# State-space stage of a hybrid decoder: decays spread over the partitions by DMA and masked on GpSimd, in place of one-hot and mask matmuls

## The chip, the cores and the metric

The kernel runs on one core of a Trainium2 chip. The metric is the device time of one execution in microseconds (us), the median of several runs. The core's engines run side by side, each through its own fixed order of instructions: TensorE (PE in the profile, its weight loads PEld), VectorE (DVE), ScalarE (ACT), GpSimd (POOL) and SyncE (SP), which issues nearly all DMAs. SBUF is the memory on the core with 128 partitions, PSUM the one that matmuls write.

## What is computed

The reference is a decoder trunk of two layers on 512 tokens with 1024 features: a Mamba-2 mixer with a dense mixer, and a sparse attention with a dense mixer. The change lies in the Mamba-2 mixer, in the scan over chunks of 256 tokens:

```python
def step(state, inp):
    xk, bk, ck, dtk = inp
    acs = jnp.cumsum(dtk * A, axis=1)
    seg = acs[:, :, None, :] - acs[:, None, :, :]
    decay = jnp.exp(jnp.where(causal[None, :, :, None], seg, -jnp.inf)).reshape(bsz, L, L, G, J)
    xdt = (xk * dtk[..., None]).reshape(bsz, L, G, J, p_dim)
    cb = jnp.einsum("blgn,bsgn->blsg", ck, bk)
    y_intra = jnp.einsum("blsg,blsgj,bsgjp->blgjp", cb, decay, xdt)
    y_inter = jnp.einsum("blgn,bgjpn->blgjp", ck, state) * jnp.exp(acs).reshape(bsz, L, G, J)[..., None]
    ...
```

There are 32 heads of 64 features in four groups, and two chunks. For each head and chunk the matrix `decay` holds exp(acs[target] - acs[source]) for all targets that are not before their source. The factor exp(acs[target]) of `y_inter` is wanted for the second chunk alone, since the state starts at zero.

## The kernel before

The kernel is written with a tile framework: the program names tiles from pools with a fixed number of buffers and the operations on them, and the framework puts the instructions of each engine into a fixed order, sets the waits and gives out buffers. All matrices of weights come from memory in units of 128 x 1024 (`Weights`, `split_unit`, lines 41 to 127): SP issues the load into one of four `raw` buffers, ACT copies it to the upper part (L112), DVE subtracts for the lower part (L113), and each unit feeds 24 matmuls of 512 columns (`mm3`, L133 to L135): an eighth of the unit by three products each.

`mamba` (line 517) makes the input projection for the steps and the first five tiles of group 0, and then goes through four groups `g` of eight heads. For each group it projects six tiles (B, C and four tiles of x, each of two heads), puts them through the convolution, and calls `ssd` (line 595). In group 0 the generator `steps` (line 454) makes, beside this, the cumulated decays `acs` of all heads with tokens on partitions, their negatives `nacs`, and `acsT`: 64 rows, the decays of the 32 heads split exactly into an upper part and a lower part, each with all 512 tokens (transposes L511, copy L514).

In `ssd` the exponent acs[target] - acs[source] is needed with sources on partitions and targets along the free dimension. The part -acs[source] is a column and is the bias of the exponential. The part acs[target] is a row that all 128 partitions need, and here PE spreads it: a matmul with a column of the one-hot matrix `oh`, repeated 128 times, as weights and `acsT` as the moving side writes the row of head `hd` into all partitions of a PSUM bank `sa` (L645, 512 columns), and once more its second halves of the chunks into a bank `sb` (L650, 256 columns). The causal mask, 0 or -1e30, is added to the diagonal blocks by four more matmuls of an identity with `mask_t` in bf16 (L647 and L652). ACT then takes four exponentials from PSUM into the tile `m` (L656 twice 256 columns, L659 twice 128), and DVE multiplies `m` by `cb`, the product of C and B (L661). `m` is what PE multiplies by the inputs `xd` (L667, L671). For the state's part, L674 multiplies state and C, and L675 spreads the two heads' rows of the second chunk over 64 partitions each, with weights `ohp`, for the exponential L677. This goes on in four pairs of heads `j`; ahead of a pair's last steps its gate is projected (`gate`, 24 matmuls, L592). Then come the norm and the splits, and after group 3 the output projection (`project_out`, L276 to L278).

Tiles of up to 4 KB a partition come from the pool `b4` with 33 buffers (`big`), smaller ones from `t2` with 8 (`tmp`). All loads of weights, of modulation rows (`mod`, L159) and of x are issued by SP in one order.

Of the kernel before, what the change touches and what calls it, by code (L numbers as in the profile page):

```python
# [9 lines left out]
F32 = mybir.dt.float32  # L10
F32R = mybir.dt.float32r
# [6 lines left out]
P = 128  # L18
S = 512
# [21 lines left out]
class Weights:  # L41
    """A matrix as a stream of 128x128 blocks, eight to a transfer, each split exactly in two."""
# [21 lines left out]
    def held(self):  # L64
        """The next eight blocks, to be kept for longer."""
        assert self.left == 0
        hi, lo = self.kern.split_unit(self.dram[self.unit], held=True)
        self.unit += 1
        return [(hi[:, i * P:(i + 1) * P], lo[:, i * P:(i + 1) * P]) for i in range(8)]


class Kernel:
# [19 lines left out]
    def banks(self, n, i=0):  # L92
        """n banks to accumulate in; of two or four, the ones of i differ."""
# [14 lines left out]
    def split(self, hi, lo, src, bias=None):  # L108
        """hi + lo is src (+ bias) with all of its bits, each part exact in float32r."""
# [27 lines left out]
    def linear(self, weights, x, ps=None):  # L137
        """One tile of 128 output features; x is a list of (hi, lo) per input tile."""
# [6 lines left out]
    def linear_start(self, weights, x, count, parts):  # L145
        """The first tiles of output features, token part by token part, as their inputs come."""
# [8 lines left out]
    def mod(self, n, behind=False):  # L155
        """Modulation columns 128 n.. : silu(c) @ mod_w + mod_b."""
# [17 lines left out]
    def scale_cols(self, gain, mod0, plus):  # L174
        """gain * (plus + modulation) as columns."""
# [5 lines left out]
    def rsqrt(self, sums, n):  # L181
        """1 / sqrt(sums / n + eps) of a few columns."""
# [20 lines left out]
    def rstd(self, sums, n):  # L203
        """1 / sqrt(mean + eps) of sums of squares [feature lane, token], on all partitions, in PSUM."""
# [10 lines left out]
    def unit_rows(self, x, out):  # L215
        """out[t] = x[t] * rstd, for a few tiles of tokens [token, feature]; written over with squares before."""
# [16 lines left out]
    def turned(self, xn, k, count=1):  # L233
        """Feature tiles k.. of rows, with features on partitions, in PSUM."""
# [8 lines left out]
    def modulate(self, h, src, scale, shift, k, sl):  # L243
        """h = (hi, lo) of src * scale + shift."""
# [8 lines left out]
    def rows(self, cols):  # L253
        """Columns of features as rows of 1024, on all partitions."""
# [17 lines left out]
    def mm3_rows(self, ps, x, t, wh, wl, start, stop):  # L272
        """Adds to ps, [token, 512 features], what input tile x gives for token tile t."""
# [6 lines left out]
    def project_out(self, dram, x, x_src, gain, x_dst, first=None, after=None, mods=(), held=()):  # L280
        """x_src + gain * rmsnorm(x @ weights), [token, feature]. The second half of the features is done in two
        token parts, and what follows on a part (after) goes on while the other is multiplied. Without first, both
        halves of the features are."""
# [29 lines left out]
        for i in range(2):  # L313
# [19 lines left out]
            # one token tile ends before the other  # L333
# [62 lines left out]
    def before(self, gain, mod0, keep=None):  # L396
        """What follows on the residual stream: the modulated norm, to go on with; and its tiles."""
# [46 lines left out]
    def conv(self, ps, j):  # L444
        """Causal convolution of four taps of channel tile j."""
# [8 lines left out]
    def steps(self, ps, c):  # L454
        """softplus, cumulated decays and what hangs on them, from the raw steps [32 heads, tokens]."""
# [45 lines left out]
        sp = self.tmp((P, 4, 2, 32), F32R)  # L501
        nc.scalar.activation(sp[:, :, 0], acs, AF.Copy)
        nc.vector.tensor_tensor(out=sp[:, :, 1], in0=acs, in1=sp[:, :, 0].bitcast(F32), op=OP.subtract)
# [6 lines left out]
        for b in range(4):  # L510
            nc.tensor.transpose(pt[0:64, b * P:(b + 1) * P], sp[:, b].rearrange("p a h -> p (a h)").bitcast(F32),  # L511
                                self.ident)
        self.acsT = self.keep.tile([64, 512], F32R, name="acsT")
        nc.scalar.activation(self.acsT, pt[0:64, :], AF.Copy)  # L514
        self.dt = dt

    def mamba(self, x, x_src, x_dst):
        nc = self.nc
        with ExitStack() as es:
            self.keep = es.enter_context(self.tc.tile_pool(name="ssm", bufs=1))  # L520
            c = self.constants(CST_M, "cst_m")
            self.mask_t = self.keep.tile([P, P], BF16, name="mask_t")
# [664 lines left out]
```

## Time and profile before

| | before |
|---|---|
| median of 3 runs | 1565.19 us (1564.48 to 1568.77) |
| span of the profiled execution | 1564.4 us |
| PE busy | 1515.3 us, 97% |
| DVE busy | 989.5 us, 63% |
| ACT busy | 701.9 us, 45% |
| POOL busy | 20.4 us, 1% |
| DMA | 226.11 MB, mean 145 GB/s |

The profile gives the span, from the first instruction to the last, as the time of its own execution. Matmuls overlap each other, so that the busy time of a group of matmuls is more than the time it keeps PE; the distance between two starts tells that. The groups' idle time is the time that their engine stood still ahead of them, with who ended the wait.

### The profile page before, as it was taken

What the parts mean: (1) busy time and instruction counts of PE and PEld (TensorE: products, weight loads), DVE (VectorE), ACT (ScalarE), POOL (GpSimd) and SP (SyncE); (2) the same over time, 40 slices, a digit from 0 to 9 for tenths busy, and PEclk for the clock granted to TensorE, in tenths of its full rate; (3) what the DMA queues carried; (4) which work ended last, traced back from release to release, by engine and by line L of the source; (5) the groups of instructions that cost most, each with busy time, mean ns of one, the idle gap of its engine ahead of it and who ended that gap; (6) DMA issues with size and microseconds to landing.
All of it is one profiled execution on the core that took longest, in us unless ns stands there. A gap on an engine that the chain in (4) does not pass through costs nothing.

```text
span 1564.4 us, 20765 instructions
## 1 busy us (share of the span) xinstructions
PE 1515.3 (97%) x8014; PEld 1216.9 (78%) x8014; DVE 989.5 (63%) x1800; ACT 701.9 (45%) x1228; POOL 20.4 (1%) x27
## 2 busy tenths in 40 slices
PE   6999999999999999999999989999999999999997
PEld 4767676777889788888878877777688888888886
DVE  7856676778585788872367578888856333333246
ACT  4564746565364222322356465655645332222243
POOL 0000000000000000000000100000000000000000
PEclk9999999999999999999999999999999999999999
DMA  8422141334763888873466443122144122232254
GB/s 303 152 68 68 41 135 46 117 121 156 257 211 109 280 296 285 297 269 101 167 215 210 108 149 94 48 75 68 42 175 149 41 95 94 95 106 95 95 202 148
DMA packets 65125, 226.11 MB, mean 145 GB/s; under 512 B 7809, under 2 KB 9345, under 8 KB 65026
## 3 DMA queue, kind: packets, MB, share of 16 engines
q1 hardware_dynamic: 64738, 224.53, 43.5%
q8 instruction: 63, 1.03, 0.3%
q14 instruction: 36, 0.29, 0.1%
q10 hardware_dynamic: 288, 0.25, 0.1%
HBM read 204.83 MB, written 8.39 MB: 136 GB/s over the span
## 4 chain that ended last, share of the span: by engine, by line
PE 77%; DVE 9%; DMA 8%; ACT 3%; issue 2%; SPq 1%; POOL 0%; DVEq 0%; ACTq 0%; POOLq 0%
PE acc L133 12%; PE acc L134 12%; PE acc L135 12%; PE seg L276 5%; PE seg L278 5%; PE seg L277 5%; PE acc L278 3%; PE acc L276 3%; PE acc L277 3%; DMA raw<-in_mod_dram 2%; DMA raw<-in_ffn_in_dram 2%; DVE w L113 2%; PE mi L1036 2%; DMA b<-b 2%; PE acc L1053 2%
## 5 line engine op out<-in xcount | busy, mean ns | idle before, releaser
L113 DVE TENSOR_TENSOR w<-raw,w 128x1024 fp32r<-128x1024 f32 x233 | 288.0, 1237 | 260.0 <-ACT w L112 259.3
L112 ACT ACTIVATE w<-raw 128x1024 fp32r<-128x1024 f32 x233 | 245.9, 1057 | 369.4 <-PE seg L278 120.5
L133 PE MATMUL acc<-b,w 128*128 128x512 f32 x976 | 386.0, 397 | 3.2 <-DVE t L450 1.0
L134 PE MATMUL acc<-b,w 128*128 128x512 f32 x976 | 384.0, 393 | 0.0
L135 PE MATMUL acc<-b,w 128*128 128x512 f32 x976 | 383.5, 393 | 0.1
L133 PEld LDWEIGHTS acc<-b,w 128*128 128x128 f32 x976 | 183.3, 188 | 43.1 <-issue 4.1
L135 PEld LDWEIGHTS acc<-b,w 128*128 128x128 f32 x976 | 183.7, 188 | 39.8 <-issue 1.7
L134 PEld LDWEIGHTS acc<-b,w 128*128 128x128 f32 x976 | 183.8, 188 | 36.9 <-issue 0.7
L160 DVE SCALAR_TENSOR_TENSOR raw<-raw,b 128x1024 f32<-128x1024 f32 x112 | 136.1, 1221 | 19.1 <-DMA raw<-in_mod_dram 18.4
L276 PE MATMUL seg<-w,b 128*128 128x512 f32 x340 | 132.9, 391 | 0.0
L278 PE MATMUL seg<-w,b 128*128 128x512 f32 x340 | 132.7, 390 | 0.0
L277 PE MATMUL seg<-w,b 128*128 128x512 f32 x340 | 132.4, 389 | 0.0
L1005 ACT ACTIVATE b<-seg,nm 128x512 f32<-128x512 f32 (+3 forms) x128 | 66.0, 525 | 52.5 <-DVE nm L1000 49.8
L112 ACT ACTIVATE b<-t 128x512 fp32r<-128x512 f32 (+1 forms) x108 | 55.2, 529 | 47.8 <-DVE t L426 38.5
L277 PEld LDWEIGHTS seg<-w,b 128*128 128x128 f32 x340 | 63.8, 188 | 13.3
L278 PEld LDWEIGHTS seg<-w,b 128*128 128x128 f32 x340 | 63.8, 188 | 13.2
L276 PEld LDWEIGHTS seg<-w,b 128*128 128x128 f32 x340 | 63.9, 188 | 12.7
L426 DVE TENSOR_TENSOR t<-t,acc 128x512 f32<-128x512 f32 x40 | 27.4, 685 | 63.3 <-PE acc L135 63.3
L425 ACT ACTIVATE t<-acc 128x512 f32<-128x512 f32 x40 | 23.7, 593 | 95.3 <-PE acc L135 95.3
L113 DVE TENSOR_TENSOR b<-t,b 128x512 fp32r<-128x512 f32 (+1 forms) x108 | 59.2, 567 | 9.2 <-ACT b L112 8.9
L277 PE MATMUL acc<-w,b 128*128 128x512 f32 x164 | 64.0, 390 | 0.0
L278 PE MATMUL acc<-w,b 128*128 128x512 f32 x164 | 64.0, 390 | 0.0
(300 smaller groups left out, 2390.1 us busy)
## 6 DMA issues: line engine op xcount, KB each, us to landing
raw<-in_mod_dram SPq DMA_DIRECT2D x112, 512.0 KB, 4.5
raw<-in_ffn_in_dram SPq DMA_DIRECT2D x88, 512.0 KB, 4.5
raw<-in_ffn_out_dram SPq DMA_DIRECT2D x66, 512.0 KB, 3.3
raw<-in_ssm_in_dram SPq DMA_DIRECT2D x41, 512.0 KB, 3.4
raw<-in_ssm_out_dram SPq DMA_DIRECT2D x24, 512.0 KB, 4.3
b<-b SPq DMA_DIRECT2D x32, 256.0 KB, 4.5
raw<-in_kv_dram SPq DMA_DIRECT2D x12, 512.0 KB, 4.2
raw<-in_q_dram SPq DMA_DIRECT2D x9, 512.0 KB, 5.5
```

The lines of the kernel that those rows point to most:

```text
L112: nc.scalar.activation(hi, src, AF.Copy)
L113: nc.vector.tensor_tensor(out=lo, in0=src, in1=hi.bitcast(F32), op=OP.subtract)
L133: nc.tensor.matmul(ps, wh, xh, start=start, stop=False)
L134: nc.tensor.matmul(ps, wh, xl, start=False, stop=False)
L135: nc.tensor.matmul(ps, wl, xh, start=False, stop=stop)
L160: i = nc.vector.scalar_tensor_tensor(out=raw, in0=raw, scalar=1.0, in1=self.cs, op0=OP.mult, op1=OP.mult, accum_out=self.modc[:, n:n + 1])
L276: nc.tensor.matmul(ps, x[0][:, ts], wh, start=start, stop=False)
L277: nc.tensor.matmul(ps, x[0][:, ts], wl, start=False, stop=False)
L278: nc.tensor.matmul(ps, x[1][:, ts], wh, start=False, stop=stop)
L1005: nc.scalar.activation(p[i], bank[:, at:at + n], AF.Exp, bias=nm[:, i:i + 1], accum_out=d[:, i:i + 1])
L1036: nc.tensor.transpose(ps[:, i * n + a * P:i * n + (a + 1) * P], unit["p"][j * per + i][:, a * P:(a + 1) * P], self.ident)
L1053: self.nc.tensor.matmul(po[64 * i:64 * i + 64, bs], vt[a][:, r * 256 + kv * 64:r * 256 + kv * 64 + 64], unit["w"][2 * i + r][:, a * P:(a + ...
```

## The change

The one-hot matrix, `ohp`, `acsT` and the bf16 mask go. `steps` transposes `acs` itself into 32 rows, copies them to `at` and stores them in memory (`acsd`, 32 x 512, 64 KB). A new function `exponents` makes, for a head, a tile of 768 columns: SP loads the head's row of 512 tokens from memory onto all 128 partitions (256 KB written), and GpSimd makes two adds of 256 elements each, the second halves of the chunks with the mask into columns 512 to 767, and the first halves with the mask in place. `ssd` calls it for the first two heads at its start and for the pair j + 1 at the start of pair j. The four exponentials of a head then go from this tile into itself. The rows for the state's part are loaded for the whole group into one tile `ea` (two loads of 64 partitions with 4 KB each) and put through one exponential of 1024 columns. The pools keep their sizes; the mask now stays in the tile of constants. Comments that the diff also takes out are left out here.

```diff
@@ steps
-        sp = self.tmp((P, 4, 2, 32), F32R)
-        nc.scalar.activation(sp[:, :, 0], acs, AF.Copy)
-        nc.vector.tensor_tensor(out=sp[:, :, 1], in0=acs, in1=sp[:, :, 0].bitcast(F32), op=OP.subtract)
...
-            nc.tensor.transpose(pt[0:64, b * P:(b + 1) * P], sp[:, b].rearrange("p a h -> p (a h)").bitcast(F32),
-                                self.ident)
-        self.acsT = self.keep.tile([64, 512], F32R, name="acsT")
-        nc.scalar.activation(self.acsT, pt[0:64, :], AF.Copy)
+            nc.tensor.transpose(pt[0:32, b * P:(b + 1) * P], acs[:, b], self.ident)
+        at = self.tmp((32, 512))
+        nc.scalar.activation(at, pt[0:32, :], AF.Copy)
+        self.acsd = self.dram.tile([32, S], F32, name="acsd")
+        nc.sync.dma_start(self.acsd, at)
@@ mamba
-            self.mask_t = self.keep.tile([P, P], BF16, name="mask_t")
-            nc.vector.tensor_copy(out=self.mask_t, in_=c("mask_t"))
-            self.oh = self.keep.tile([64, 32], F32R, name="oh")
-            nc.scalar.activation(self.oh, c("onehot")[0:64], AF.Copy)
@@ new
+    def exponents(self, hd, c):
+        nc = self.nc
+        e = self.big((P, 768))
+        nc.sync.dma_start(e[:, 0:512], self.acsd[hd:hd + 1, :].to_broadcast([P, 512]))
+        v = e[:, 0:512].rearrange("p (k b l) -> p k b l", k=2, b=2)
+        mask = c("mask_t")[:, None, :].to_broadcast([P, 2, P])
+        nc.gpsimd.tensor_tensor(out=e[:, 512:768].rearrange("p (k l) -> p k l", k=2), in0=v[:, :, 1], in1=mask,
+                                op=OP.add)
+        nc.gpsimd.tensor_tensor(out=v[:, :, 0], in0=v[:, :, 0], in1=mask, op=OP.add)
+        return e
@@ ssd
+        es = [self.exponents(8 * g + i, c) for i in range(2)]
+        ea = self.big((P, 4, 256))
+        for i in range(2):
+            nc.sync.dma_start(ea[64 * i:64 * i + 64],
+                              self.acsd[8 * g + i:8 * g + 8:2, 256:512][None].to_broadcast([64, 4, 256]))
+        nc.scalar.activation(ea, ea, AF.Exp)
...
-        ohp = self.tmp((64, 8, 64), F32R)
-        nc.scalar.activation(ohp, self.oh[:, 8 * g:8 * g + 8, None].bitcast(F32).to_broadcast([64, 8, 64]), AF.Copy)
-        ohp = ohp.rearrange("p (j i) d -> p j (i d)", i=2)
...
-            sb = self.seg()
-            for i in range(2):
+            now = es
+            es = [self.exponents(8 * g + 2 * j + 2 + i, c) for i in range(2)] if j < 3 else []
+            for i, m in enumerate(now):
                 hd = 8 * g + 2 * j + i
-                sa = self.seg()
-                oh = self.oh[:, hd:hd + 1].to_broadcast([64, P])
-                nc.tensor.matmul(sa, oh, self.acsT, start=True, stop=False)
-                for k in range(2):
-                    nc.tensor.matmul(sa[:, k * 256:k * 256 + P], self.identb, self.mask_t, start=False, stop=k == 1)
-                v = sb[:, i * 256:(i + 1) * 256].rearrange("p (k l) -> p k l", k=2)
-                a2 = self.acsT.rearrange("p (k b l) -> p k b l", k=2, b=2)[:, :, 1]
-                nc.tensor.matmul(v, oh, a2, start=i == 0, stop=False, skip_group_check=True)
-                for k in range(2):
-                    nc.tensor.matmul(v[:, k], self.identb, self.mask_t, start=False, stop=k == 1,
-                                     skip_group_check=True)
-                m = self.big((P, 768))
-                for k in range(2):
-                    nc.scalar.activation(m[:, k * 256:(k + 1) * 256], sa[:, k * 256:(k + 1) * 256], AF.Exp,
-                                         bias=self.nacs[:, 2 * k, hd:hd + 1])
-                for k in range(2):
-                    nc.scalar.activation(m[:, 512 + k * P:512 + (k + 1) * P], v[:, k], AF.Exp,
-                                         bias=self.nacs[:, 2 * k + 1, hd:hd + 1])
+                for at, n, b in ((0, 256, 0), (256, 256, 2), (512, 128, 1), (640, 128, 3)):
+                    nc.scalar.activation(m[:, at:at + n], m[:, at:at + n], AF.Exp, bias=self.nacs[:, b, hd:hd + 1])
                 nc.vector.tensor_tensor(out=m, in0=m, in1=cb, op=OP.mult)
...
-            nc.tensor.matmul(pi[:, 256:512], ohp[:, j], self.acsT[:, 256:512], start=True, stop=True)
-            ea = self.tmp((P, 256))
-            nc.scalar.activation(ea, pi[:, 256:512], AF.Exp)
-            nc.vector.tensor_tensor(out=ea, in0=ea, in1=pi[:, 0:256], op=OP.mult)
+            nc.vector.tensor_tensor(out=ea[:, j], in0=ea[:, j], in1=pi[:, 0:256], op=OP.mult)
```

## Rows read from the trace of the kernel before

**Rows 1.** The page: the span, and in 40 slices PE busy and its granted clock.

```profile
span 1564.4 us, 20765 instructions
...
PE   6999999999999999999999989999999999999997
...
PEclk9999999999999999999999999999999999999999
```

**Rows 2.** The chain that ended last, 86 to 385 us: shares by line.

```profile
by line: PE acc L134 19.1%; PE acc L133 19.0%; PE acc L135 19.0%; PE mi L667 7.9%; PE seg L645 4.1%; PE mi L674 3.4%; PE seg L650 3.1%; PE mi L671 2.9%; PE mi L620 2.5%; PE seg L652 2.3%; PE mi L630 2.3%; PE seg L647 2.2%; PE mi L675 1.7%; 
```

**Rows 3.** Groups of instructions of PE, 86 to 385 us: line, operands, count | busy, mean | idle before.

```profile
L133 PE MATMUL acc<-b,w 128*128 128x512 f32 x248 | 99.5, 401 | 1.0 <-DVE t L450 1.0
```

**Rows 4.** Stretches: length, busy us (count) of PE, PEld, DVE, ACT, POOL; clock, DMA share, GB/s.

```profile
155.40:239.10 83.70, 83.70 (x407) 60.16 (x406) 57.58 (x93) 49.19 (x82) 0.00 (x0) 1.00 0.27 88
155.40:202.10 46.70, 46.70 (x238) 30.52 (x236) 26.99 (x38) 33.34 (x63) 0.00 (x0) 1.00 0.12 42
...
322.90:369.80 46.90, 46.90 (x244) 31.42 (x242) 36.43 (x59) 34.44 (x63) 0.00 (x0) 1.00 0.41 132
369.80:400.00 30.20, 30.20 (x144) 25.14 (x144) 25.94 (x54) 11.72 (x15) 0.32 (x1) 1.00 0.61 202
```

**Rows 5.** Instructions of PE in order of time, from 123 us: start, length, line.

```profile
123.03 0.50 PE L645 MATMUL seg<-acsT,oh 64*128 64x512 f32 x1
123.45 0.28 PE L647 MATMUL seg<-mask_t,identb 128*128 128x128 bf16 x2
123.67 0.38 PE L650 MATMUL seg<-acsT,oh 64*128 64x256 f32 x1
123.98 0.28 PE L652 MATMUL seg<-mask_t,identb 128*128 128x128 bf16 x2
124.20 0.49 PE L645 MATMUL seg<-acsT,oh 64*128 64x512 f32 x1
```

**Rows 6.** The same, from 343.9 us: the first of six, and the next head's.

```profile
343.92 0.50 PE L645 MATMUL seg<-acsT,oh 64*128 64x512 f32 x1
...
344.79 0.38 PE L650 MATMUL seg<-acsT,oh 64*128 64x256 f32 x1
```

**Rows 7.** The same, around the first L675.

```profile
97.30 0.38 PE L675 MATMUL mi<-acsT,t 64*128 64x256 f32 x1
97.52 0.39 PE L645 MATMUL seg<-acsT,oh 64*128 64x512 f32 x1
```

**Rows 8.** Instructions of ACT in order of time, 81 to 90 us.

```profile
81.95 0.58 ACT L514 ACTIVATE acsT<-mi 64x512 fp32r<-64x512 f32 x1
...
88.63 0.84 ACT L656 ACTIVATE b<-seg,nacs 128x256 f32<-128x256 f32 x2
89.36 0.63 ACT L659 ACTIVATE b<-seg,nacs 128x128 f32<-128x128 f32 x2
```

**Rows 9.** DMA issues: tiles, engine, count, size of each, median us to landing.

```profile
out_dram<-b SPq DMA_DIRECT2D x8, 256.0 KB, 2.0
b<-b SPq DMA_DIRECT2D x32, 256.0 KB, 4.5
b<-t SPq DMA_DIRECT2D x16, 64.0 KB, 2.0
```

**Rows 10.** Instructions of POOL and DVE in order of time, near 882 and 979 us.

```profile
881.96 1.63 POOL L706 TENSOR_TENSOR t<-t,b 128x512 f32<-128x512 f32 x1 [2.87 <-DVE t L705]
882.36 2.31 DVE L113 TENSOR_TENSOR w<-raw,w 128x1024 fp32r<-128x1024 f32 x1
...
978.78 1.28 POOL L706 TENSOR_TENSOR t<-t,b 128x512 f32<-128x512 f32 x1 [24.73 <-DVE t L705]
```

**Rows 11.** Instructions of PE in order of time: the first products of the first pair.

```profile
96.09 0.65 PE L667 MATMUL mi<-b,b 128*64 128x256 f32 x2
```

**Rows 12.** Groups of instructions of DVE, 155.4 to 239.1 us: splits of weights and products.

```profile
L113 DVE TENSOR_TENSOR w<-raw,w 128x1024 fp32r<-128x1024 f32 x10 | 12.2, 1217 | 0.0
L661 DVE TENSOR_TENSOR b<-b,b 128x768 f32<-128x768 f32 x8 | 7.7, 957 | 8.5 <-ACT b L659 8.5
```

More of the change, by code (lines that the diff above doesn't have):

```diff
@@ L683, in ssd @@
                                            op0=OP.mult, op1=OP.add)
-            nc.vector.tensor_tensor(out=y[:, 256:512], in0=y[:, 256:512], in1=ea, op=OP.add)
+            nc.vector.tensor_tensor(out=y[:, 256:512], in0=y[:, 256:512], in1=ea[:, j], op=OP.add)
             z = zs[j] if j < len(zs) else self.gate(w, h, self.tmp())
@@ L1078 @@
                      ("dt_bias", 1), ("pe_k", 16), ("pe_v", 16)])
-CST_M, _ = _places([("tri", 128), ("mask_t", 128), ("onehot", 32)])
+CST_M, _ = _places([("tri", 128), ("mask_t", 128)])
 CST_A, _ = _places([("mask_q", 128), ("add_pe", 128), ("cmp_add", 128), ("cmp_ok", 128)])
@@ L1087, in _constants @@
     ok = ((16 * cc + 31 <= t) & (cc < 31)).reshape(P, 128)
-    m = [i[:, None] <= i[None, :], np.where(i[:, None] <= i[None, :], 0.0, NEG),
-         i[:, None] % 32 == np.arange(32)[None, :]]
+    m = [i[:, None] <= i[None, :], np.where(i[:, None] <= i[None, :], 0.0, NEG)]
     q = [np.where(i[None, :] <= i[:, None], 0.0, NEG), np.eye(P) + (i[:, None] == 31), np.where(ok, 0.0, NEG), ok]
```

## The prediction

> **What bounds the kernel now.** I read the page first. The span is 1564.4 us, and the median of the runs shown is 1565.19, so the profiled execution stands for them within 0.8 us and I make the sum against 1565. The row of TensorE (PE) in the 40 slices stands at 9 nearly everywhere, and its granted clock at 9 throughout, the upper of its two levels [rows 1]. That is only a busy share, so the next view is the chain of waits, cut to the state-space stage, 86 to 385 us: if the matmuls that the change removes lie on the chain there, their time is worth its full amount. They do. L645, L650, L652, L647 and L675 hold 4.1 + 3.1 + 2.3 + 2.2 + 1.7 = 13.4% of these 299 us, 40.1 us [rows 2]. The grouped view of the same stretch says how idle PE was: one of its 25 groups of matmuls shows idle time ahead of it, 1.0 us, waiting for VectorE (DVE), and the others show none [rows 3]. So here PE sets the end, and it never waits for what the change makes faster or slower. The third view is the stretches by engine. One group of eight heads takes 83.7 us, with PE busy in all of it, DVE in 57.58 and ScalarE (ACT) in 49.19. Inside it the part with the heads (155.4 to 202.1) is 46.7 us, with ACT at 33.34 [rows 4]. These are the loads that must still fit once PE is shorter.
>
> **What is removed on PE.** For each of the 32 heads go one 512-column and one 256-column matmul against the one-hot rows and four bf16 mask matmuls; for each of the 16 pairs of heads goes the 256-column product with ohp. Matmuls overlap, so a duration is no price; the price is the distance between starts. Where the six run in one piece, the next head's L645 starts at 124.20 after 123.03: 1.17 us [rows 5]. Where PE comes from other work and goes on, the six take 343.92 to 344.79: 0.87 us [rows 6]. L675 takes 97.30 to 97.52: 0.22 us [rows 7]. So 32 x 0.87 + 16 x 0.22 = 31.4 us, or 32 x 1.17 + 3.5 = 40.9 us. The chain says 40.1. I take 38, nearer the chain, since it counts all of them in their places. The four transposes of steps stay (32 rows in place of 64).
>
> **What is removed elsewhere.** On ACT: a copy and a split per group and the four exponentials of L677, which one 1024-column exponential per group replaces; on DVE one subtraction of the split. I price these at nothing, since PE is late there and not these engines. The 32 x 4 exponentials keep their sizes and read SBUF in place of PSUM; two of 256 columns take 0.84 us and two of 128 take 0.63, 1.47 us a head [rows 8].
>
> **What is added.** (1) One 64 KB store of the cumulated decays, 32 loads of 256 KB that repeat a 2 KB row on 128 partitions, and eight more of 256 KB (two a group, 64 partitions each) for ea, all on SP's queue. The bytes are 40 x 256 KB = 10.5 MB over the 299 us, 35 GB/s on top of the 42 to 202 GB/s that its stretches move, at a DMA share of 0.12 to 0.61 [rows 4], so the engines have room. What counts is latency: a 64 KB load landed after 2.0 us, 256 KB ones after 2.0 and 4.5 us [rows 9]. No row shows a row repeated from memory; the bounds are 2.0 and 4.5 and I take the later one, as that form is also a load to SBUF. (2) Two adds of 256 elements on GpSimd (POOL) per head, 64 in all. The only adds before are 512 wide and took 1.28 us at their shortest and 1.63 us in the case that the first rival looks at [rows 10]. Bounds: half of the former, 0.64, and the whole, 1.28; I take 0.7, because half the elements is the nearer row. The Trainium skill, GPSIMD Engine Reference, section 4.1, advises against adds on GpSimd, about twice as slow as VectorE; its 4497 ns for 2048 elements with the 1.28 us above gives an estimate of 0.74 us, and the sum would be the same. With 0.7, POOL works 16 x 0.7 = 11 us of a group of some 75 us, and is no bound by itself.
>
> **What the path pays.** In the first group the decays come later. Now acsT is ready at 81.95 + 0.58 = 82.53. The store (2.0), the load (4.5), two adds of the first head (1.4), its exponentials (1.5) and its product (0.96) make 10.4 us: 92.9, and the second head another 1.5, by ACT; the present first product of the pair starts at 96.09 [rows 8, 11]. The removed matmuls of three heads (3 x 1.17 = 3.5 us) lie ahead of that, so PE would want to start it near 92.6: 0 to 3 us late, with gate matmuls as cover. I take 1. In the later groups the pair of heads ahead is loaded while the present one is multiplied (some 9 us), against 4.5 + 2.8 us for load and adds; cover holds, price nothing. If it failed it would cost that chain, below. What SP has queued behind a waiting load are weight loads; they have four raw and three split buffers, up to seven units ahead of PE with 24 matmuls each, so a wait of some us is covered. Then the tighter fit: with 38/4 = 9.5 us less in a group, ACT has 33 us in a part of 37 us, and DVE 27 us plus what GpSimd holds up. PE's order is fixed and it will wait now and then; I put 1.5 us a group on this, 6 in all. It is bounded by nothing and by the second rival. Last, in the fourth group DVE is already at 36.43 of 46.9 and then 25.94 of 30.2 us [rows 4]; I add 1 us for GpSimd there.
>
> Sum: 1565 - 38 + 1 + 6 + 1 = 1535 us.
>
> **Rivals.** *VectorE and GpSimd take turns, and VectorE becomes the bound (slower).* The trace shows the mechanism: with a GpSimd add from 881.96 to 883.59, the split L113, which starts at 882.36, takes 2.31 us where its mean in the state-space group is 1.22; it ends 1.08 us after the add [rows 10, 12]. The Trainium skill, SBUF — State Buffer, section "SBUF: two separate sides", calls this an exclusive lock for the whole instruction between GpSimd and a VectorE instruction with two SBUF inputs; the trace agrees, 2.31 against 1.22 us. Here ten such splits and eight products a group take 12.2 + 7.7 us, with smaller ones besides [rows 12], so an add meets one perhaps half the time. If every add stopped DVE for its whole length p, a group would need 57.58 + 16p: 68.8 us at 0.7, still below PE's 74; it reaches the present 83.7 at p = 1.63, the contended price of an add twice as wide. At that p the first three groups gain nothing and the last stretch, 322.9 to 400, needs 36.43 + 25.94 + 26 = 88 in place of 77.1: +11, or 1576 us. Over all four the loss overtakes the gain from p = 1.45 on: 3 x (83.7 - 57.58 - 16p) + (77.1 - 62.37 - 16p) is zero there. Against it: half the width, and half the meetings.
>
> *The part with the heads stays bound by ScalarE's chain (half the gain).* ACT is busy 33.34 of 46.7 us there; if PE runs out of gate matmuls and the next group's are not moved in, the part shrinks only to about 42 us in place of 37: 4 x 4.5 = 18 us of the 38 are lost, and 1565 - 38 + 18 + 2 = 1547. For it: the exponentials, squares, gates and splits share ACT, and all of PE's cover is in a fixed order. Against it: exponentials no longer wait for PE at all.
>
> *The full gain.* If nothing waits, 1565 - 40 = 1525.
>
> *The prefetch does not happen.* The shared pool of 33 big tiles now holds ea, the constants and two more pairs of heads for longer. If the next pair waits for the present one's tiles, the chain per pair is 4.5 + 2.8 + 2.9 + 1.9 = 12.1 us against 9 of PE, and four of them 48.4 us, in place of 46.7 now: 1565 + 4 x 1.7 = 1572 if it is so everywhere. In the last group alone, where most tiles are held, it loses 9.5 + 1.7: 1535 + 11 = 1546.
>
> **How the numbers follow.** Forecast 1535 with its own range 1528 to 1542: 0.50. Half the gain or a prefetch lost in the last group, 1542 to 1558: 0.25. The full gain, 1523 to 1528: 0.09. Within 0.3% of 1565, about what a measurement of this kernel can tell from no change (1560.5 to 1569.9), by a larger share of the same losses: 0.06. Slower, by VectorE or the prefetch: 0.10. So faster 0.84, same 0.06, slower 0.10, and 1524 to 1556 holds 8 in 10.
>
> **What would show it.** Right: the stretch from the first head group to the last is some 30 us shorter, PE still at 9 in its slices, POOL with 64 adds near 0.7 us, everything behind 400 us merely shifted. Lock: products and splits of the stage well above 0.957 and 1.217 us, and idle PE time ahead of the matmuls that read the products, put down to DVE. ScalarE: PE idle put down to ACT within the heads. Prefetch: GpSimd waiting on DMA each pair, and SP waiting on the products. The forecast is wrong if added PE idle time in the stage exceeds 15 us, or if code behind the stage falls into another order.

## The result, and the profile after

The changed kernel takes 1555.4 us (median of 4 runs, 1552.1 to 1556.5) beside 1564.8 us for the kernel before on the same chip: a ratio of 0.9933, interval 0.9909 to 0.9956. That is 10 us faster, a third of the 30 us forecast. It lies outside the forecast's own range (1528 to 1542) and just inside the upper end of the wide one (1524 to 1556).

The page of the changed kernel (its span; TensorE and GpSimd in 40 slices) against [rows 1]:

```profile
span 1554.3 us, 20592 instructions
...
PE 1485.1 (96%) x7806; PEld 1204.2 (77%) x7806; DVE 997.8 (64%) x1798; ACT 710.3 (46%) x1216; POOL 83.2 (5%) x91
...
PE   6999899999999999999999999999999999999998
...
POOL 0040303040000000000000100000000000000000
```

Among the first nine slices, which hold the stage, one 8 in the row of PE is all that the page shows; GpSimd's busy time now stands in four of the first nine slices, one for each group of heads. The gain is made within the stage and stays: the first matmul of the next projection, L276, starts at 355.9 us in place of 365.8, and the last matmul of all at 1546.2 in place of 1555.9.

The chain that ended last, 81 to 378 us, shares by line (the view cuts its own line), against [rows 2]:

```profile
by line: PE acc L133 11.5%; PE acc L134 11.3%; PE acc L135 11.0%; DMA b<-acsd 7.1%; PE mi L664 5.2%; issue 4.2%; DVE w L113 2.6%; DVE b L680 2.4%; DVE raw L160 2.3%; DVE b L658 2.3%; DVE b L676 2.2%; DVE t L450 2.2%; DMA raw<-in_mod_dram 2.
```

The three lines of the linear matmuls fell from 57% to 34% of the chain. It was PE alone; now it runs through VectorE and the loads of the rows as well, so TensorE alone no longer sets the end.

Groups of TensorE's instructions, 76 to 376 us (line, operands, count | busy, mean ns | idle before, and what ended it), against [rows 3]:

```profile
L133 PE MATMUL acc<-b,w 128*128 128x512 f32 x248 | 102.2, 412 | 10.0 <-ACT w L112 4.3 <-DVE t L450 2.5 <-ACT t L587 2.3
...
L664 PE MATMUL mi<-b,b 128*64 128x256 f32 x128 | 31.0, 391 | 3.5 <-DVE b L658 3.0 <-issue 0.4
...
L208 PE MATMUL mi<-ones,ssq 128*128 128x1 f32 x32 | 5.6, 297 | 2.8 <-DVE ssq L684 2.8
```

The idle time ahead of L133 went from 1.0 to 10.0 us, and most of it waits for ScalarE: for the split of weights (L112) and for a gate (L587).

Stretches of the second group of heads (length, busy us of PE, PEld, DVE, ACT, POOL; clock, DMA share, GB/s), against the first two of [rows 4]:

```profile
149.20:231.60 82.40, 76.54 (x356) 57.91 (x355) 59.12 (x93) 51.45 (x80) 14.59 (x16) 0.96 0.40 122
149.20:191.20 42.00, 38.82 (x199) 27.30 (x197) 28.29 (x40) 37.36 (x62) 14.59 (x16) 1.00 0.35 97
```

The part with the heads shrank by 4.7 us, but ScalarE is busy in 37.36 of its 42.0 us, where it had 33.34 of 46.7. The whole group shrank by only 1.3 us, and the granted clock is no longer 1.00 in it.

Of the 4.0 us that ScalarE has more, 3.8 are table loads, 10 in place of 7 (one stands wherever ScalarE goes over between a Silu and the exponentials). The groups of its instructions in that part, before (155.4 to 202.1 us) and after (149.2 to 191.2):

```profile
L656 ACT ACT_TABLE_LOAD x3 | 3.8, 1283 | 0.1
L592 ACT ACT_TABLE_LOAD x3 | 3.8, 1283 | 0.1
...
L659 ACT ACT_TABLE_LOAD x1 | 1.3, 1283 | 0.0
```

```profile
L657 ACT ACT_TABLE_LOAD x4 | 5.1, 1283 | 0.1
L587 ACT ACT_TABLE_LOAD x4 | 5.1, 1283 | 0.1
...
L573 ACT ACT_TABLE_LOAD x1 | 1.3, 1283 | 0.0
L612 ACT ACT_TABLE_LOAD x1 | 1.3, 1283 | 1.0 <-DMA b<-acsd 1.0
```

Here is the end of that part, TensorE first, then ScalarE (start, length, line, [idle before <- what ended it]):

```profile
188.70 0.38 PE L668 MATMUL mi<-b,b 128*64 128x128 f32 x2
191.24 0.50 PE L133 MATMUL acc<-b,w 128*128 128x512 f32 x1 [2.16 <-ACT w L112]
191.58 0.39 PE L134 MATMUL acc<-b,w 128*128 128x512 f32 x1
193.39 1.87 PE L208 MATMUL mi<-ones,ssq 128*128 128x1 f32 x8 [1.42 <-DVE ssq L684]
195.12 0.77 PE L133 MATMUL acc<-b,w 128*128 128x512 f32 x1
195.70 0.63 PE L134 MATMUL acc<-b,w 128*128 128x512 f32 x1
196.12 0.63 PE L135 MATMUL acc<-b,w 128*128 128x512 f32 x1
```

```profile
178.52 1.28 ACT L587 ACT_TABLE_LOAD   x1
179.81 0.60 ACT L587 ACTIVATE t<-acc 128x512 f32<-128x512 f32 x1
180.43 1.28 ACT L657 ACT_TABLE_LOAD   x1
181.72 1.20 ACT L657 ACTIVATE b<-b,nacs 128x256 f32<-128x256 f32 x3
183.95 0.63 ACT L682 ACTIVATE t<-b 128x512 f32<-128x512 f32 x1 [1.02 <-DVE b L680]
184.49 1.77 ACT L657 ACTIVATE b<-b,nacs 128x128 f32<-128x128 f32 x5
186.17 0.61 ACT L112 ACTIVATE b<-b 128x512 fp32r<-128x512 f32 x1
186.80 1.28 ACT L587 ACT_TABLE_LOAD   x1
188.09 0.60 ACT L587 ACTIVATE t<-acc 128x512 f32<-128x512 f32 x1
188.59 1.66 ACT L112 ACTIVATE b<-b 128x512 fp32r<-128x512 f32 x3
190.14 1.04 ACT L112 ACTIVATE w<-raw 128x1024 fp32r<-128x1024 f32 x1
```

ScalarE works in its program's order. The split of the next weights (the last line, started at 190.14) stands behind the exponentials, a gate and three other splits, and TensorE's L133 starts at 191.24 with 2.16 us of idle time. Every switch between the gate's Silu and the exponentials costs a table load of 1.28 us. Then the sum of squares is late too, and after these two gaps the same matmuls start 0.42 us apart (195.70, 196.12), where they are 0.24 us apart at the full clock (L134's 63.7 us over 261 in the kernel before). The stretches around it, same columns, give the clock:

```profile
192.80:199.60 6.80, 6.21 (x19) 5.24 (x20) 5.57 (x15) 1.29 (x2) 0.00 (x0) 0.50 0.48 156
199.60:206.40 6.80, 6.80 (x33) 5.58 (x32) 3.84 (x6) 1.73 (x2) 0.00 (x0) 1.00 0.24 77
```

0.50 is the lower of the two levels, 1.2 GHz: 19 matmuls in 6.8 us against 33 in the next 6.8.

A balance of the stage can be made from the distances between the starts of TensorE's instructions, from the first L133 after 74 us to the first L276. It took 291.3 us before and 281.8 after, 9.5 less:

- the removed matmuls held 12.7 (L645) + 4.9 (L647) + 9.7 (L650) + 4.8 (L652) + 4.1 (L675) = 36.2 us;
- idle time in gaps of over 0.15 us rose from 1.5 to 19.0, by 17.4 us;
- in stretches at the lower clock, none before and 18.8 us after, the instructions took 8.3 us more than the same forms take at the full clock.

-36.2 + 17.4 + 8.3 = -10.5; 1.0 us is left. It hides two terms that nearly cancel, by the same distances. The 32 products L674, which had L675 behind them, take 3.6 us less (10.1 to 6.5 us), so that the removal is worth 39.8 us in all, near the 40.1 us that the chain of waits gave. And up to the first L276 the change gets through 24 more of the other matmuls, some 4 us.

One of the low stretches, 73.4 to 76.8 us, lies ahead of the heads, where both kernels have the same matmuls (see the last section); 2.7 of the 18.8 us are its.

What was added, as groups of GpSimd's instructions (80 to 370 us) and DMA issues (76 to 376 us; size, median us to landing):

```profile
L600 POOL TENSOR_TENSOR b<-b,b 128x256 f32<-128x256 f32 x32 | 33.7, 1052 | 0.0
L598 POOL TENSOR_TENSOR b<-b,b 128x256 f32<-128x256 f32 x32 | 31.0, 968 | 280.0 <-DMA b<-acsd 277.0 <-DVE b L641 2.7
```

```profile
b<-acsd SPq DMA_DIRECT2D x40, 256.0 KB, 5.8
...
acsd<-t SPq DMA_DIRECT2D x1, 64.0 KB, 3.8
```

GpSimd and VectorE do take turns. Instructions in order of time, GpSimd, then VectorE, near 106 and 160 us:

```profile
106.54 0.74 POOL L598 TENSOR_TENSOR b<-b,b 128x256 f32<-128x256 f32 x1
...
160.12 0.73 POOL L600 TENSOR_TENSOR b<-b,b 128x256 f32<-128x256 f32 x1
160.81 1.50 POOL L598 TENSOR_TENSOR b<-b,b 128x256 f32<-128x256 f32 x1
```

```profile
106.56 1.53 DVE L658 TENSOR_TENSOR b<-b,b 128x768 f32<-128x768 f32 x1
...
160.77 0.96 DVE L658 TENSOR_TENSOR b<-b,b 128x768 f32<-128x768 f32 x1 [0.65 <-issue]
```

An add alone takes 0.73 us. One that starts 0.04 us after a product of 0.96 us takes 1.50, near the product's rest plus its own 0.73. The other way round it is the product that is stretched: one that starts 0.02 us after an add takes 1.53 us. Over the stage the 32 products take 1.013 us in the mean, against 0.957 [rows 12].

### The profile page after: what moved, and what is told of

It is laid out like the page before. It is cut to its first block, busy times and chain, and to the rows that moved or that the text cites. A ratio compares the mean times of both kernels' runs of the same rounds, so it can differ in the third digit from the quotient of the medians.

```text
span 1554.3 us, 20592 instructions
## 1 busy us (share of the span) xinstructions
PE 1485.1 (96%) x7806; PEld 1204.2 (77%) x7806; DVE 997.8 (64%) x1798; ACT 710.3 (46%) x1216; POOL 83.2 (5%) x91
## 4 chain that ended last, share of the span: by engine, by line
PE 66%; DVE 13%; DMA 10%; issue 5%; ACT 4%; POOL 1%; SPq 1%; DVEq 0%; ACTq 0%; POOLq 0%
PE acc L133 10%; PE acc L134 10%; PE acc L135 10%; PE seg L277 5%; PE seg L278 5%; PE seg L276 5%; DMA raw<-in_mod_dram 3%; PE acc L277 3%; PE acc L278 3%; PE acc L276 3%; DVE w L113 2%; DVE raw L160 2%; DMA raw<-in_ffn_in_dram 2%; PE mi L1030 2%; DMA b<-b 2%
## 5 line engine op out<-in xcount | busy, mean ns | idle before, releaser
L113 DVE TENSOR_TENSOR w<-raw,w 128x1024 fp32r<-128x1024 f32 x233 | 289.1, 1242 | 259.9 <-ACT w L112 259.3
L112 ACT ACTIVATE w<-raw 128x1024 fp32r<-128x1024 f32 x233 | 245.8, 1057 | 373.0 <-PE seg L278 121.2
L133 PE MATMUL acc<-b,w 128*128 128x512 f32 x976 | 388.8, 399 | 12.5 <-ACT w L112 4.9
L134 PE MATMUL acc<-b,w 128*128 128x512 f32 x976 | 385.1, 395 | 0.8 <-DVE b L113 0.8
L135 PE MATMUL acc<-b,w 128*128 128x512 f32 x976 | 385.1, 395 | 0.1
L133 PEld LDWEIGHTS acc<-b,w 128*128 128x128 f32 x976 | 184.6, 190 | 55.7 <-ACT w L112 6.1
L135 PEld LDWEIGHTS acc<-b,w 128*128 128x128 f32 x976 | 184.9, 189 | 40.6 <-issue 1.6
L134 PEld LDWEIGHTS acc<-b,w 128*128 128x128 f32 x976 | 185.3, 190 | 39.5 <-DVE b L113 1.9
L276 PE MATMUL seg<-w,b 128*128 128x512 f32 x340 | 132.7, 391 | 0.0
L112 ACT ACTIVATE b<-t 128x512 fp32r<-128x512 f32 (+1 forms) x108 | 55.1, 529 | 49.2 <-DVE t L426 39.5
L276 PEld LDWEIGHTS seg<-w,b 128*128 128x128 f32 x340 | 63.9, 188 | 13.0
L276 PE MATMUL acc<-w,b 128*128 128x512 f32 x164 | 64.0, 392 | 1.6 <-ACT w L112 1.6
L113 DVE TENSOR_TENSOR b<-t,b 128x512 fp32r<-128x512 f32 (+1 forms) x108 | 59.1, 567 | 8.4 <-ACT b L112 8.2
```

Of the source, the lines that this page charges most:

```text
L112: nc.scalar.activation(hi, src, AF.Copy)
L113: nc.vector.tensor_tensor(out=lo, in0=src, in1=hi.bitcast(F32), op=OP.subtract)
L133: nc.tensor.matmul(ps, wh, xh, start=start, stop=False)
L134: nc.tensor.matmul(ps, wh, xl, start=False, stop=False)
L135: nc.tensor.matmul(ps, wl, xh, start=False, stop=stop)
L276: nc.tensor.matmul(ps, x[0][:, ts], wh, start=start, stop=False)
```

## The experiments

Three theories. S: ScalarE's queue, fuller by table loads and in a fixed order, lets TensorE idle at the ends of the parts with the heads, and the clock falls there. V: GpSimd's adds hold up the products and VectorE. D: the rows of decays arrive late. Each run is compared by its ratio to the kernel before on its own chip; “idle” and “clock” are the two terms of the balance above, and “tables” the table loads from 80 to 370 us (lines of the groups of ScalarE's instructions, summed). Idle and clock are those of one profiled execution each, up to the first L276, and executions of one kernel differ: the four of e2 run from 1543.25 us, at a mean granted clock of 0.996, to 1553.19 at 0.989.

| run | median, us | ratio [95%] | idle, us | clock, us | tables |
|---|---|---|---|---|---|
| kernel before | 1564.8 | 1 | 1.5 | 0 | 27 |
| the change | 1555.4 | 0.9933 [0.9909, 0.9956] | 19.0 | 8.3 | 34 |
| e1, no masks | 1549.1 | 0.9891 [0.9861, 0.9921] | 16.1 | 7.4 | 34 |
| e2, splits earlier | 1546.8 | 0.9888 [0.9855, 0.9921] | 14.5 | 7.2 | 34 |
| e3, gates by Exp | 1542.4 | 0.9861 [0.9833, 0.9888] | 14.9 | 1.3 | 15 |
| e4, no rows | 1543.6 | 0.9855 [0.9822, 0.9887] | 11.6 | 2.8 | 28 |
| e5, gates by Tanh | 1542.0 | 0.9848 [0.9826, 0.9869] | 15.0 | 3.0 | 15 |
| e6, e5 and e2 | 1548.9 | 0.9890 [0.9871, 0.9908] | 14.6 | 8.4 | 15 |
| e7, e3 and e1 | 1534.9 | 0.9793 [0.9773, 0.9813] | 6.5 | 1.4 | 15 |
| e8, e3 and e4 | 1531.6 | 0.9782 [0.9759, 0.9806] | 6.9 | 3.3 | 15 |
| e9, adds aside | 1539.3 | 0.9818 [0.9803, 0.9833] | 10.4 | 1.5 | 15 |
| e10, adds on VectorE | 1548.0 | 0.9875 [0.9855, 0.9894] | 11.6 | 5.2 | 13 |
| e11, before with Tanh | 1569.3 | 1.0015 [1.0001, 1.0029] | 0.9 | 0 | 9 |
| e12, before without masks | 1552.6 | 0.9905 [0.9888, 0.9921] | 1.3 | 0 | 28 |

**e1: no adds on GpSimd.** The exponentials read the loaded rows directly, those of 128 columns first; `nacs` changes its sign, here and in e4, e7, e8, e9 and e12 (left out of the cuts).

```diff
-        nc.gpsimd.tensor_tensor(out=e[:, 512:768]..., in0=v[:, :, 1], in1=mask, op=OP.add)
-        nc.gpsimd.tensor_tensor(out=v[:, :, 0], in0=v[:, :, 0], in1=mask, op=OP.add)
```

> The changed kernel without the two GpSimd adds of each head: the exponentials read the loaded rows as they are (no causal mask, and the sources' part enters with the other sign so that nothing overflows; the output is not the decoder's). Changed kernel: 1555.4 us. Theory S (ScalarE's queue is late at the end of each group's heads: exponentials, table loads, then the split of the next weights; TensorE then idles and its granted clock falls): 1551 to 1557, since ScalarE keeps all its work. Theory V (GpSimd's adds hold up VectorE's products and splits): the products fall from 1013 to 957 ns, the other stretched groups too, and the time to 1545 or less. Theory D (latency of the loads from memory, 5.8 us median): about 1550 to 1556, the chain is shorter by the adds alone.

0.9891: 0.0042 below the change, 6.6 us of 1565, though the two intervals overlap. The 1549.1 us lie between the band of S (from 1551) and that of V (up to 1545), and just below D's (from 1550). TensorE still waits 4.1 us for the split L112 and 2.2 for the gate L587 ahead of L133, as in the change: without the adds ScalarE is as late as with them. The products fall to 0.953 us, as V has it, but the time does not fall that far: V is at most a part.

**e2: the splits of weights ahead of the exponentials.**

```diff
             mh = []
+            if j >= len(zs) - 1:
+                while len(w.queue) < 2 and w.unit < 41:
+                    w.prefetch()
             now = es
```

> The changed kernel, with the loads and splits of the next two units of weights written ahead of each pair of heads, so that ScalarE's and VectorE's part of the split stands earlier in their orders. Theory S: the idle stretches of TensorE at the end of the heads (2.2 + 1.4 + 1.2 us in groups 1 and 2, like ones in 0 and 3, 16 us in all) mostly go, the clock stays at 1.00 in the 10 us slices there, and the time is 1541 to 1549. Theories V and D: 1553 to 1557, the products are no earlier.

0.9888, 7 us below the change, with intervals that overlap a little. The waits of L133 for L112 are gone from the groups (7.6 us left, on VectorE's L450, the gate and L448), and 4.5 us of idle time with them. Moving one split forward helps, but the gate still stands behind exponentials, and the clock still falls (7.2 us).

**e3: gates by the exponentials' own function,** so that ScalarE needs no other table between them.

```diff
-        self.nc.scalar.activation(out, ps, AF.Silu)
+        self.nc.scalar.activation(out, ps, func)     # Exp for the gates among the heads
```

> The changed kernel with the four gates of a group put through the exponential instead of Silu (the output is not the decoder's), so that ScalarE needs no table switch between a gate and the exponentials of the heads: some 6 to 8 loads of 1.28 us fewer in each of groups 1 to 3. Theory S: ScalarE is through some 8 us earlier per group, the idle of TensorE at the end of the heads mostly goes: 1541 to 1548. Theories V and D: 1553 to 1557.

0.9861: 11.3 us better than the change, more than e1 or e2 bring, and clear of the change's interval. Table loads fall from 34 to 15, 19 x 1.283 = 24 us of ScalarE's time. TensorE's idle time falls by only 4.1 us and the clock's cost by 7.0: the gaps in the change that end the part with the heads (2.16 and 1.42 us, twice) and precede the two longest stretches at the lower clock are gone; what is left are mainly short waits for the products (L664, at most 1.78 us) and two of 2.40 us for a convolution (L450).

**e4: no loads, no adds.** The removal alone: the exponentials read a constant of the same size.

```diff
-        nc.sync.dma_start(e[:, 0:512], self.acsd[hd:hd + 1, :].to_broadcast([P, 512]))
-        (both adds of e1, the two loads of ea)
-                    nc.scalar.activation(m[:, at:at + n], m[:, at:at + n], AF.Exp, bias=...)
+                    nc.scalar.activation(m[:, at:at + n]..., mask_t broadcast, AF.Exp, bias=...)
```

> The changed kernel without the spread rows: no loads of rows, no adds on GpSimd; the exponentials (same sizes and number) read the constant mask tile, the sources' part enters with the other sign (the output is not the decoder's). It is the removal of the matmuls alone. Theory S: ScalarE keeps all its work, so most of the loss stays: 1545 to 1553. Theories V and D: nothing is left that holds TensorE, nearly all 36 to 40 us come: 1526 to 1532.

0.9855, a gain of 22.7 us of the 36.2 removed; 1543.6 us is just below the band of S (from 1545) and far from that of V and D. Even with all the added work gone, over a third of the removed time does not arrive. So about half of the change's shortfall of 25.7 us, 13.5, is not what it adds; it lies in what it leaves in place, in an order and with table loads (28, not 34) that are not quite the change's.

**e5: a gate that computes the same with Tanh,** silu(z) = 0.5 z (1 + tanh(z/2)); its output is the reference's. The factor 0.5 goes into the product behind it, which is left out here.

```diff
+        self.nc.scalar.activation(out, ps, AF.Tanh, scale=0.5)
+        self.nc.vector.scalar_tensor_tensor(out=out, in0=out, scalar=1.0, in1=ps, op0=OP.add, op1=OP.mult)
```

> The changed kernel with the gates' Silu written as 0.5 z (1 + tanh(z / 2)), tanh on ScalarE and one more product on VectorE: the same result without a switch of tables between a gate and the heads' exponentials. Theory S: about as with the exponential in place of Silu (1542.4 us), less what the 13 more VectorE products cost (13 x 0.75 = 10 us of VectorE, some of it beside other work): 1541 to 1547; table loads in the stage fall from 34 to about 15. Theory V (VectorE held up by GpSimd sets the end): VectorE gets more work, so 1555 or later.

0.9848: 1542.0 us, the fastest version here that computes the reference, ahead of both kernels. ScalarE's table loads in the stage, before the edit and after it:

```profile
L587 ACT ACT_TABLE_LOAD x14 | 18.0, 1283 | 0.2
L657 ACT ACT_TABLE_LOAD x13 | 16.7, 1283 | 0.2
```

```profile
L663 ACT ACT_TABLE_LOAD x4 | 5.1, 1283 | 0.1
...
L587 ACT ACT_TABLE_LOAD x1 | 1.3, 1283 | 0.0
```

13 of those ahead of the exponentials become 4, and the 14 ahead of a gate become 1. The Trainium skill, ScalarE: Activation LUTs, section "Table sets: the hidden batching unit", lists tanh beside exp in one set and advises to batch calls by set; the trace agrees, with 15 loads in place of 34. The Trainium skill, ScalarE: Activation LUTs, section "What ACT_TABLE_LOAD costs", puts a switch at about 2.66 us with a drain behind the load; here the activation starts 1.29 us after the load does (178.52, 179.81), so the trace's 1.28 us decides.

**e6: e5 and e2 together.**

> The gates by tanh and the early splits together. Theory S: both causes of the same idle stretches, so the gains (13 and 9 us) don't add up: 1536 to 1543. Theory V: no better than 1553.

0.9890, slower than e5 alone, and a miss: I had expected 1536 to 1543 us, no worse than e5. The idle time is that of e5 (14.6 against 15.0 us). The clock's term is 8.4 us against 3.0, and the largest stretch is at the end of the first group, after one gap (TensorE in order of time):

```profile
119.70 0.79 PE L133 MATMUL acc<-b,w 128*128 128x512 f32 x1 [3.51 <-DVE t L593]
120.29 0.63 PE L134 MATMUL acc<-b,w 128*128 128x512 f32 x1
```

```profile
118.60:128.80 10.20, 9.06 (x24) 7.00 (x25) 6.13 (x19) 3.21 (x4) 0.00 (x0) 0.50 0.17 53
```

e5 has the same gap of 3.51 us, up to 119.1. There the matmuls behind it still run at the full clock, and 6.8 us at the lower one begin at 121.0, at a second gap; here 10.2 us begin at 118.6, within the gap, and 3.4 us each follow near 214 and 293 us. The clock's 5.4 us are most of the 6.6 us by which the two ratios differ, if the profiled executions stand for the others. Why the clock falls earlier and for longer after an equal gap, no run here settles.

**e7: e3 and e1 together. e8: e3 and e4 together.**

> Gates by the exponential, and in addition no GpSimd adds (no causal mask, the sources' part with the other sign; the output is not the decoder's). It is the price of GpSimd where ScalarE is relieved. Theory S alone: 1540 to 1543, no change against 1542.4. If GpSimd's hold on VectorE is a second limit behind ScalarE: 1532 to 1538; without the mask and with ScalarE loaded it was worth 1555.4 - 1549.1 = 6 us.

> Gates by the exponential, no rows loaded and no adds on GpSimd, the exponentials read the constant mask (the output is not the decoder's): the removal of the matmuls alone, with ScalarE relieved. Theory S: what was missing in the removal alone (1543.6 against the 1526 to 1532 of a full gain) was ScalarE's: 1527 to 1534. If VectorE or TensorE's order holds the rest: 1538 to 1543.

0.9793 and 0.9782. Only with the switches gone and the adds gone does almost all of the removed time arrive: 0.0218 x 1565 = 34.1 us of 36.2 (39.8 with L674) in e8. From there the shortfall can be put together in both orders. Silu put back first: e8 to e4, 11.4 us; then the loads, e4 to e1, 5.6; then the adds, e1 to the change, 6.6. Loads first: e8 to e7, 1.7; then adds, e7 to e3, 10.6; then Silu, e3 to the change, 11.3. The switches cost the same in both orders, the adds 7 to 11 us, and the loads 2 to 6 us. A step is uncertain by some 5 to 7 us, so that the two figures of 11 us agree so closely is luck; the smaller step of the adds and both steps of the loads are not clear of the intervals. S is the largest part in one order and level with V in the other; D is the smallest.

**e9: the adds aside.** e7 with 64 GpSimd adds of the same size put back, for whose results nobody waits.

```diff
                 mh.append(m)
+                for q in range(2):
+                    nc.gpsimd.tensor_tensor(out=self.spare[:, q], in0=v[:, :, q], in1=mask, op=OP.add)
```

> The gates as exponentials and the exponentials without the masks, as in the run before that gave 1534.87 us, but the 64 GpSimd adds are put back with their sizes and operands: they read the finished weights of a head and write a tile that nobody reads, so nothing waits for their results (the output is not the reference's). Two forms of the theory on GpSimd. Lock: the adds cost by stretching VectorE's instructions with two SBUF operands, so most of the 7.6 us come back: 1540 to 1544, products of the weights near 1.0 us. Latency: they cost because the exponentials wait for them, so nothing comes back: 1533 to 1537.

0.9818, between the two forms: 3.9 of the 10.6 us come back, though the intervals of e7 and e9 overlap a little.

```profile
L660 POOL TENSOR_TENSOR spare<-b,b 128x256 f32<-128x256 f32 x64 | 72.3, 1160 | 259.8 <-DVE b L655 249.5 <-issue 9.3 <-POOL spare L660 0.9
```

These adds met VectorE more than the change's did (1160 ns in the mean, against 968 and 1052), and the products took 1.166 us. So taking turns alone is worth some 4 us. The other 7 us I put down to latency: in e3 the exponentials wait 19.2 us for the adds (11.4 and 7.8 by the groups of ScalarE's instructions), in e9 not at all; in the change, where ScalarE is itself late, they wait only 4.0. No run takes the latency out alone.

**e10: the adds on VectorE,** behind the products of the pair before, with e5's gates.

```diff
-        nc.gpsimd.tensor_tensor(... OP.add)
+            for e in es:
+                self.masked(e, c)      # the same two adds, on nc.vector
```

> The tanh gates (1542.0 us with GpSimd's adds) with the 64 mask adds on VectorE, placed behind the products of the pair of heads before. Lock: VectorE gets 64 x some 0.35 us = 22 us of its own work but loses the stretching and the turns; products back at 0.95 us, time 1535 to 1541. If it is only VectorE's load that counts and not the turns: 1542 to 1547, since its load in the stage is then as large as with the stretching.

0.9875, 4 us slower than e5 by the ratios (1545.4 of 1565), but their intervals overlap: no gain is shown, and no loss. The first expectation falls, and the second holds by the ratio; the median, 1548.0, is 1 us above it. The form of V that counts only turns would have made this a gain.

```profile
L668 DVE TENSOR_TENSOR b<-b,b 128x768 f32<-128x768 f32 x32 | 30.4, 954 | 0.3 <-ACT b L667 0.2
...
L607 DVE TENSOR_TENSOR b<-b,b 128x256 f32<-128x256 f32 x32 | 13.5, 422 | 2.5 <-DMA b<-acsd 2.5
L609 DVE TENSOR_TENSOR b<-b,b 128x256 f32<-128x256 f32 x32 | 13.5, 421 | 0.0
```

The products are back at 0.954 us, the turns are gone, and VectorE has 27 us of adds of its own instead (0.42 us each, where I had estimated 0.35). The table's idle time is 3.4 us below e5's, but in this run the first L276 stands ahead of the stage's last 76 matmuls. Just behind it, at 336.6, TensorE waits 2.56 us more for a split on VectorE (L113), with 3.4 us at the lower clock from there. So the idle time is 14.2 us against e5's 15.0, and the clock's term is above by more than the table's 2.2 us.

**e11: the kernel before with e5's gates.**

> The kernel before with tanh in place of Silu for the gates of the heads. ScalarE's table loads fall as they did after the change, but here TensorE never waits for ScalarE in the stage. Theory S (ScalarE's chain binds only once TensorE is shorter): 1562 to 1567, no gain. If the table loads cost time in any version: 1552 to 1556, the 11 us that they gave after the change.

1.0015 (1.0001 to 1.0029): no gain, if anything a small loss, and just above the expected band. Stretches from 80 to 370 us, the kernel before and e11:

```profile
80.00:370.00 290.00, 288.98 (x1425) 204.08 (x1424) 199.11 (x321) 170.53 (x299) 0.04 (x1) 1.00 0.27 89
```

```profile
80.00:370.00 290.00, 289.33 (x1415) 201.28 (x1414) 205.23 (x330) 146.06 (x280) 0.32 (x1) 1.00 0.27 86
```

ScalarE lost 24.5 us of work and nothing got faster, since TensorE is full in both. The same edit gives 13 us after the change (0.9933 to 0.9848). This is the clearest evidence for S: the table loads are free while TensorE is late, and cost time once it is not.

**e12: the kernel before without the mask matmuls,** one part of the removal alone.

```diff
-                    nc.tensor.matmul(sa[:, k * 256:k * 256 + P], self.identb, self.mask_t, ...)
-                    nc.tensor.matmul(v[:, k], self.identb, self.mask_t, ...)
```

> The kernel before without the 128 mask matmuls (its decays have the sign flipped, so the output is not the reference's); the one-hot rows stay on TensorE. Distance between starts is 0.22 us for each two, 32 x 0.44 = 14 us; the chain of waits says 13.5. A heads part of 46.7 us becomes 43.3, still above ScalarE's 33 with some room. Theory S: this smaller part of the removal arrives nearly whole, 1550 to 1554. Rival, that ScalarE's limit binds from the first us: a gain in the changed kernel's proportion (10 of 36.5), 4 us, 1559 to 1562.

0.9905: 14.9 us, all of the 14 us expected, with 1.3 us of idle time and no fall of the clock. The balance has only 9.7 us at the masks themselves (L647 and L652); the one-hot matmuls beside them took 4.4 us less as well (L645 12.7 to 10.6, L650 9.7 to 7.4, by the same distances). The first 14 us of the removal arrive whole; the change, which removes 36.2, keeps 10.5. So the limit is no proportion. It fits a point that lies between, which e4 and e8 put at ScalarE: the same removal gives 22.7 us with its table switches and 34.1 without.

## Why the prediction was wrong

- *What bounds the kernel.* Right: TensorE, alone. e11 shows it from the other side.
- *What is removed on PE.* Right: 38 us put down, 36.2 measured by the distances between starts, 39.8 with what L674 gave up, and 34.1 us of gain when the adds, the loads and the switches are out of the way (e8).
- *What is removed elsewhere.* The first step that failed. The prediction kept ScalarE's 33 us in the part with the heads and put the savings at nothing. Its load rose from 33.34 to 37.36 us in the second group, and 3 x 1.283 = 3.8 us of this are table loads, 10 in place of 7. In the whole stage they went from 27 to 34. They were there to be read in the trace of before, and the prediction counts none. The exponentials of 256 and of 128 columns also rose, from 476 and 366 ns to 498 and 388.
- *What is added.* Adds alone 0.73 us, against 0.7; in the kernel 0.97 and 1.05, by turns, inside the bounds. The store took 3.8 and the loads 5.8 us, against 2.0 and 4.5: above both bounds. This delayed nothing at the first pair (95.85 us in place of 96.09, [rows 11]), where the prediction put 1 us. For the later pairs it put nothing, “cover holds”, and that failed too: the adds are worth 7 to 11 us (e1, e3 against e7), the loads 2 to 6 (e8 to e7, e4 to e1).
- *What the path pays.* The term that was mis-sized: 1 + 6 + 1 = 8 us against 17.4 of idle time and 8.3 of clock. “1.5 us a group” was a guess for a part in which ScalarE would be busy 33 of 37 us, 89%. The 37.36 of 42.0 us that came are the same share, so the tightness was in view; what was missing is that ScalarE's fixed order put the split of the next weights behind the last exponentials and a gate, where TensorE waits for it. The price of the lower clock after such gaps was missing altogether.
- *The rivals.* The one on ScalarE's chain was the right mechanism for nearly half of the loss (11 of 25.7 us), with the right place. That the part with the heads took 42.0 us, as it said, is partly luck, since it had ScalarE at 33 us there. It gave 1547 in place of 1555: the gaps at the end of that part and behind it, and the lower clock that follows them, were not in it. Taking turns exists as described, but its price is some 4 us (e9), and the adds' 0.97 and 1.05 us are far from the 1.45 us an add at which it would have turned the sign. The prefetch does happen, though GpSimd waits 277 us on DMA, a sign that the prediction named for its failing: most of that is the time ahead of the first group and between groups. In the second group the last adds end at 177.5 us and the exponentials run to 186; SP waited for the products 3.6 us in the whole stage, and e8 gains nothing that can be told from e7.
- *What would show it.* The bound given there, 15 us of added idle time, was passed at 17.4; and the waits of L133 on ScalarE are the sign named for that rival. The signs of the lock show too, but small: products at 1.013 us, splits at 1.255, and 3.0 us of TensorE's waiting for products.

## What to carry to other kernels

Before work is taken from the engine that is full, sum up the next engine over the shortened part, with its table loads, and look at what stands in its queue ahead of the operand that the full engine reads next; a part of a removal can bring as much as the whole (e12 gains 14.9 us, the change 10). Work that is free while another engine is late (the Silu switches: 0 in e11) gets its price when that engine is relieved (11 to 13 us after the change). And one limit hides the next: with the switches gone (e3), the exponentials' waiting for the adds rose from 4.0 to 19.2 us. The mask costs time on any engine here: 14.9 us on TensorE (e12), 7 to 11 on GpSimd (e1, e7), some 13 on VectorE (e10 against e7, whose gates differ).

## What of the hardware was not expected

The clock fell from 2.4 to 1.2 GHz behind gaps of only 1.4 to 3.5 us of idle time (2.16 and 1.42 us near 191 and 193, then 6.8 us at 0.50), and that added half again to what the gaps cost: in the change 8.3 us came on top of 17.4. Not every such gap does it: in e7 a gap of 2.40 us at 197.0 is followed by 3.4 us at the lower clock, and one of 2.40 us at 273.7 by none. The plainest case lies ahead of the heads, near 73 us, where all 14 traces have a gap of 1.38 to 1.40 us before the same matmul (L135, waiting for L113). In six of them (the change, e1, e2, e4, e6, e10) some 3.4 us at the lower clock follow, in the other eight none. So the length of a gap does not tell whether it costs clock, and differences of a few us between two executions can be this alone. Of a GpSimd add and a VectorE product that meet, the one that starts second pays: the add 1.50 us in place of 0.73, or the product 1.53 in place of 0.96.
